# A hybrid attention and state-space layer: one Strassen group of 14 weight pairs, the second half's indexer and attention first, rotary rows gathered by head group

## The chip, the cores and the metric

The kernel runs on one core of a Trainium2 chip. The core has a matmul engine (TensorE, in the profile PE, with its weight loads as PEld), three engines for elementwise work (VectorE or DVE, ScalarE or ACT, GpSimd or POOL), a queue engine (SyncE or SP) that issues most transfers, and 16 DMA engines that carry them. The metric is the device time of one execution in microseconds; 1805.1 us is the median of three runs before the change.

## The reference

One layer over 1024 positions of width 2048. One projection `w_in` gives queries, keys, values and a gate for sparse attention, an indexer that picks 256 keys for each query, and the inputs of a Mamba-2 mixer. Both results, 1024 wide each, are concatenated and mapped by `w_out`; a residual and a layer norm end the layer.

```python
u = jnp.einsum('bsd,de->bse', h, w_in[layer])
q, k, v, z_attn, q_idx, k_idx, w_idx, z_ssd, xbc, dt_raw = _split_cols(u, IN_WIDTHS)
q, k, q_idx, k_idx = ...            # rotary on the first quarter of each head
# for each block of 128 queries:
logits = relu(einsum('bqhd,bsd->bqhs', q_idx, k_idx))      # 16 indexer heads
score = einsum('bqhs,bqh->bqs', logits, w_idx)             # masked by chunks of 64
sel = top_k(score, 256)                                    # 8 query heads, 2 key heads
o_attn = softmax_attention(q, k[sel], v[sel]) * silu(z_attn)
# the mixer: causal convolution of 4 taps, SiLU, scan in chunks, gate, RMS norm
o_ssd = _ssd_mixer(xbc, z_ssd, dt_raw, ...)
sub = jnp.einsum('bse,ed->bsd', concat(o_attn, o_ssd), w_out[layer])
h = _layer_norm(DEEPNORM_ALPHA * h + sub, ln_g[layer], ln_b[layer])
```

All is float32. The kernel reaches that precision with three matmuls in a rounded format for each product: operand = high part + low part, and high x high, high x low and low x high are summed.

## The kernel before

**Projection (T stage).** The output columns of `w_in` are cut into tiles of 128 (`ORDER`, line 53): `misc` (indexer key, weights, time steps), `qi` (indexer queries), `k`, `v`, `q`, `z`, `xbc` and `zs`. The 1024 positions are two halves `h`, the 2048 input channels two sides `u`. A *piece* is one weight tile of 128 x 1024 (one side of a column tile) times one x set of eight 128 x 512 tiles: 8 steps of 3 matmuls into a PSUM bank `pj`. A *plain* tile takes two pieces for each half, one for each side. Columns in `GROUPS` (line 56) go through Strassen's scheme in Winograd's form instead: two column tiles are one pair, and with the two halves and two sides they take 7 pieces instead of 8, at the price of sums of weights (`T3`, `T2`), of x (`M2`, `M3`, `S1`, `S4`, formed by `t_xform`, line 772, and kept in DRAM as `xf`) and of results (`t_save`, `t_u3`, `t_comb`, lines 690 to 745). `units` (line 573) lists the pieces: 13 plain tiles (`FIRST`, `PLAIN`) for half 0 and then half 1, a group of 12 pairs (k, v, q and 6 of xbc), and a group of 8 (`z`, `zs`).

**Weights.** `w_load` (line 805) brings a raw tile (512 KB) to one of five `wr` buffers. `w_split` (853) makes the high part `wh` on ScalarE and the low part `wl` on VectorE or GpSimd (`two`, 456, picks), three buffers each, or spare `s4` tiles. Where a piece needs a sum, `w_load` brings all its raw tiles and `t_wacc` (824) adds them; a sum that a later piece needs again is stored to DRAM and loaded back. `product` (656) says which: the second piece of a pair's first phase loads B12, B22 and B11 and stores T3 and T2, the next phase loads those again.

**x.** `request` and `t_xst` (751 to 770) bring and split the eight tiles of the next x set when the one before last is used up. Their raw tiles come from the `u` buffers (27 of 2 KB a partition), which everything else uses as well.

**Indexer, attention, scan.** When a column tile is done, a task takes it on: rotary by `rope_rows` (1258), on 32 rows of a tile and so once for each of 20 tiles; `t_qi` and `t_score` (1380, 1421) the indexer; `t_topk` (1442) a bitwise search for the cut, 33 counting passes on ScalarE for each block of queries; `t_kv` and `t_attn` (1613, 1649) attention in three lanes in the order of `ATT` (line 63), half 0 first; `t_ssd` and `t_gate` (1828, 1943) the scan and its norm. Each task is a generator that says at each `Need` what it waits for.

**Output (O stage).** `mixed` times `w_out`, again by Strassen: 7 products (`PRODUCTS`, line 64) of 8 pieces, 24 matmuls to a piece. Weights that are sums are added in `t_wacc` as they are loaded, T1 and T2 stored for T2 and T4. `forms` (917) loads or forms the left operands of the next product when the third of eight pieces of the current one comes. `E_ORDER` (65) puts the mixer's rows first. `t_oevac` and `ln_apply` (2034, 2125) add residuals and do the layer norm; the eight `t_fill` transfers (2120) put `ln_b` into the output beforehand, and GpSimd's accumulating transfers add to it.

**What sets the order.** The whole order is made while the kernel is built. `Flow` (342) keeps a model (`Sim`, 124) of each engine's clock and of the buffers. Matmuls are taken in the order of `units`; between them `pump` (460) issues steps of tasks whose needs the model holds for met, lower priority numbers first. Every instruction goes to its engine in that order, and each engine works through its queue strictly. All instructions are issued through one helper, so every row of the profile has line 301, and groups are told apart by tile names: `pj<-xh,wh` and the like are T pieces (x moves), `pj<-wh,xh` O pieces (weights move), `wr` raw weights, `xt` and `xf` raw x and sums of x, `t` stored sums of weights, `mx` rows of `mixed`, `s<-s,sm` softmax exponentials.

Of the kernel before, what the change touches and what calls it, by code (L numbers as in the profile page):

```python
# [29 lines left out]
NU = 27  # L30
# [3 lines left out]
XRAW = 5  # L34
# [8 lines left out]
def tile_order():  # L43
# [28 lines left out]
def tile_cols(kind, j):  # L72
    if kind == "misc":
        return [(O_KI, 64), (O_WI, 16), (O_DT, 16)]
    base = {"qi": O_QI, "k": O_K, "v": O_V, "q": O_Q, "z": O_Z}
# [48 lines left out]
class Sim:  # L124


    LAT = 70.0

    def __init__(self):
# [4 lines left out]
        self.recent = []  # L134

# [141 lines left out]
    def dma(self, eng, out, in_, kw):  # L277
        q = {"SP": "SP", "A": "AQ", "G": "G"}[eng]
        at, notes = self.deps([out], [in_], "D")
        start = max(self.clk[q], at)  # L280
        self.clk[q] = start + (1000.0 if eng == "G" else 400.0)
        sb = in_ if in_dram(out) else out
        row = max(sb.ap[-1][1] * 4, 64)
        x = max(start + (1000 if eng == "G" else 400), self.clk["D"])
        self.clk["D"] = x + max(out.size(), in_.size()) * 4 * (1 / 400 + 0.6 / row)
        cell = [self.clk["D"] + 1500.0, start]
        self.note(notes, cell, "D")
        return cell

# [52 lines left out]
class Flow:  # L342
# [6 lines left out]
    def __init__(self, nc):  # L349
# [11 lines left out]
        self.spare = 2  # L361
        self.signals = []
# [13 lines left out]
    def avail(self, tag):  # L376
        if tag == "us":
            return self.avail("u") + max(self.avail("s4") - self.spare, 0)
        if tag == "ob":
# [3 lines left out]
    def new(self, tag, shape, dtype=F):  # L383

        if tag == "us":
            tag = "u" if self.avail("u") else "s4"
        if tag == "ob":
# [27 lines left out]
    def ready(self, task):  # L415
# [10 lines left out]
        for tag, k in n.slots.items():  # L426
            if self.avail(tag) < k + (n.keep if tag == "u" else 0):
# [112 lines left out]
class Piece:  # L540


    def __init__(self, kind, h=0, t=0, u=0, **kw):
# [3 lines left out]
        self.done = self.after = None  # L547
        self.op = ALU.add
# [3 lines left out]
class Layer:  # L552
    def __init__(self, ctx, tc, a):
# [7 lines left out]
        for tag, n in (("xh", 16), ("xl", 16), ("wr", 5), ("wh", 3), ("wl", 3), ("u", NU), ("s4", N4), ("cv", 2), ("sm", 8)):  # L561
# [11 lines left out]
    def units(self):  # L573
# [3 lines left out]
        self.sets = [("x", 0, 0), ("x", 0, 1), ("x", 1, 0), ("x", 1, 1)]  # L577
# [7 lines left out]
        def plain(h, tile, u, listed=True):  # L585
            kind, j = tile
            t = ORDER.index(tile)
            p = Piece("T", h, t, u, load=(("w", t, u),), n=2 * h + u, open=u == 0, close=u == 1, key=(h, t),
# [3 lines left out]
            put(p, listed)  # L592

        for u in range(2):
            for tile in FIRST:
                plain(0, tile, u)
        for tile in PLAIN[:-3]:
            plain(0, tile, 0)
            plain(0, tile, 1)
        for u in range(2):  # L600
            for tile in PLAIN[-3:]:
                plain(0, tile, u)
        for u in range(2):
            for tile in FIRST:
                plain(1, tile, u)
        for tile in PLAIN:
            plain(1, tile, 0)
            plain(1, tile, 1)
        a11 = 2
        for gi, pairs in enumerate(GROUPS):  # L610
            base = len(self.sets)
            if gi:
                self.sets.append(("x", 1, 0))
                a11 = base
                base += 1
            self.sets += [("f", "M2"), ("f", "M3"), ("x", 0, 1), ("f", "S1"), ("f", "S4"), ("x", 1, 1)]
# [4 lines left out]
            for ph in range(3):  # L621
                for couple in couples:
                    for f in range(2):
                        for c in couple:
                            i = put(self.product(gi, c, pairs[c], ph, f, n[ph][f]))
                            if ph and not (ph == 1 and f == 1):
                                self.hooks.setdefault(max(i - 2, 0), []).append(lambda gi=gi, c=c, ph=ph, f=f: self.pre_ld(gi, c, ph, f))
# [1567 lines left out]
```

## Time and profile before

| | us |
|---|---|
| runs | 1801.65, 1805.1, 1808.22 |
| median | 1805.1 |
| the profiled execution's own time | 1807.99 |
| its span, first to last instruction | 1806.2 |
| TensorE busy in it | 1669.0 |
| mean granted TensorE clock | 0.966 of full speed |

The page gives busy time and count for each engine, the same over 40 slices of the span (45 us each), and groups of instructions, each with its total, the mean duration of one in ns, and the idle time of its engine just before it with what ended it. A matmul's own duration (about 390 ns) is longer than its distance to the next one, as they overlap; the pace has to be read from a window in which TensorE is never idle. Windows give busy time, counts, granted clock and the share of the DMA engines for stretches that the reader chooses. The chain follows the work that ended last back to the start.

### The profile page before, as it was taken

What the parts mean: (1) busy time and instruction counts of PE and PEld (TensorE: products, weight loads), DVE (VectorE), ACT (ScalarE), POOL (GpSimd) and SP (SyncE); (2) the same over time, 40 slices, a digit from 0 to 9 for tenths busy, and PEclk for the clock granted to TensorE, in tenths of its full rate; (3) what the DMA queues carried; (4) which work ended last, traced back from release to release, by engine and by line L of the source; (5) the groups of instructions that cost most, each with busy time, mean ns of one, the idle gap of its engine ahead of it and who ended that gap; (6) DMA issues with size and microseconds to landing.
All of it is one profiled execution on the core that took longest, in us unless ns stands there. A gap on an engine that the chain in (4) does not pass through costs nothing.

```text
span 1806.2 us, 24602 instructions
## 1 busy us (share of the span) xinstructions
PE 1669.0 (92%) x8044; PEld 1371.3 (76%) x8044; DVE 1337.8 (74%) x2401; ACT 1026.4 (57%) x1858; POOL 180.0 (10%) x219
## 2 busy tenths in 40 slices
PE   9997999999999989989889899999999978998895
PEld 7985877787778778768767677878888767876684
DVE  6788878887766789978876666776676467679874
ACT  5674886655557866888544654654645433531442
POOL 0000000010000000012000110002311011200224
PEclk9998999999999999999989999999999998999898
DMA  7468733876766787775678977977689896687786
GB/s 273 164 242 270 269 130 100 314 272 237 284 230 226 239 272 237 236 275 185 250 246 288 346 233 231 341 253 270 216 285 313 270 359 238 229 294 275 236 193 93
DMA packets 211648, 447.76 MB, mean 248 GB/s; under 512 B 23872, under 2 KB 63552, under 8 KB 210496
## 3 DMA queue, kind: packets, MB, share of 16 engines
q1 hardware_dynamic: 206480, 437.41, 70.6%
q0 software_dynamic: 4608, 8.39, 3.1%
q8 instruction: 63, 1.03, 0.2%
q14 instruction: 65, 0.53, 0.1%
q10 hardware_dynamic: 432, 0.39, 0.1%
HBM read 340.85 MB, written 113.64 MB: 252 GB/s over the span
## 4 chain that ended last, share of the span: by engine, by line
PE 38%; DVE 19%; DMA 17%; issue 13%; ACT 9%; SPq 2%; POOL 2%; DVEq 0%; POOLq 0%; ACTq 0%
PE pj L301 29%; DVE u L301 8%; PE a L301 7%; DMA wr<-wt 6%; ACT u L301 5%; DVE wl L301 4%; DVE wr L301 2%; ACT wh L301 2%; SPq L301 2%; DMA wr<-wo 2%; PE o L301 2%; DVE s L301 2%; DMA u<-xfM 1%; DMA u<-xn 1%; DVE xl L301 1%
## 5 line engine op out<-in xcount | busy, mean ns | idle before, releaser
L301 PE MATMUL pj<-xh,wh 128*128 128x512 f32 (+1 forms) x1512 | 598.4, 396 | 36.3 <-ACT wh L301 13.1
L301 PE MATMUL pj<-xh,wl 128*128 128x512 f32 (+1 forms) x1512 | 585.3, 387 | 2.9 <-DVE wl L301 2.9
L301 PE MATMUL pj<-xl,wh 128*128 128x512 f32 (+1 forms) x1512 | 584.5, 387 | 0.0
L301 DVE TENSOR_TENSOR wl<-wr,wh 128x1024 fp32r<-128x1024 f32 (+2 forms) x241 | 287.2, 1198 | 154.4 <-ACT wh L301 154.2
L301 PEld LDWEIGHTS pj<-xh,wh 128*128 128x128 f32 x1512 | 290.1, 192 | 93.8 <-ACT wh L301 15.9
L301 PEld LDWEIGHTS pj<-xh,wl 128*128 128x128 f32 x1512 | 289.3, 191 | 63.9 <-DVE wl L301 6.3
L301 PEld LDWEIGHTS pj<-xl,wh 128*128 128x128 f32 x1512 | 289.8, 192 | 51.0
L301 ACT ACTIVATE wh<-wr 128x1024 fp32r<-128x1024 f32 (+2 forms) x245 | 250.8, 1031 | 132.5 <-PE pj L301 81.3
L301 PE MATMUL a<-u,u 128*128 128x512 f32 (+3 forms) x680 | 164.6, 361 | 19.4 <-DVE u L301 7.4
L301 DVE TENSOR_TENSOR u<-u,u 128x512 f32<-128x512 f32 (+9 forms) x254 | 154.5, 624 | 26.7 <-DMA u<-o 7.5
L301 DVE TENSOR_TENSOR wr<-wr,wr 128x1024 f32<-128x1024 f32 x107 | 132.8, 1241 | 54.0 <-DMA wr<-wt 32.3
L301 PE MATMUL pj<-wh,xh 128*128 128x512 f32 x366 | 148.6, 406 | 17.1 <-ACT xh L301 10.3
L301 ACT ACTIVATE xh<-u 128x512 fp32r<-128x512 f32 x170 | 101.7, 624 | 100.2 <-DVE u L301 34.9
L301 PEld LDWEIGHTS a<-u,u 128*128 128x128 f32 x680 | 114.6, 195 | 55.3 <-DVE u L301 13.4
L301 PE MATMUL pj<-wl,xh 128*128 128x512 f32 x366 | 145.7, 398 | 4.8 <-DVE wl L301 4.8
L301 ACT ACTIVATE u<-s,sm 128x640 bf16<-128x640 int16 (+7 forms) x132 | 130.2, 986 | 34.2 <-DVE sm L301 31.3
L301 PE MATMUL pj<-wh,xl 128*128 128x512 f32 x366 | 145.7, 398 | 1.6 <-DVE xl L301 1.6
L301 DVE TENSOR_TENSOR xl<-u,xh 128x512 fp32r<-128x512 f32 x168 | 110.1, 694 | 31.2 <-ACT xh L301 30.9
L301 ACT ACTIVATE u<-u 128x512 f32<-128x512 f32 (+4 forms) x161 | 91.1, 577 | 58.5 <-DVE u L301 42.3
L301 ACT ACTIVATE u<-a 128x256 fp32r<-128x256 f32 (+2 forms) x145 | 49.8, 361 | 123.0 <-DVE u L301 55.6
L301 ACT ACTIVATE a<-a 128x512 f32<-128x512 f32 (+3 forms) x160 | 75.5, 502 | 42.3 <-PE a L301 40.3
L301 PEld LDWEIGHTS pj<-wh,xh 128*128 128x128 f32 x366 | 70.5, 193 | 34.3 <-ACT xh L301 11.8
(223 smaller groups left out, 2084.6 us busy)
## 6 DMA issues: line engine op xcount, KB each, us to landing
wr<-wt SPq DMA_DIRECT2D x228, 512.0 KB, 4.9
wr<-wo SPq DMA_DIRECT2D x71, 512.0 KB, 5.7
u<-xt SPq DMA_DIRECT2D x104, 256.0 KB, 5.2
u<-u SPq DMA_DIRECT2D x100, 256.0 KB, 4.5
t<-wr SPq DMA_DIRECT2D x40, 512.0 KB, 4.3
wr<-t SPq DMA_DIRECT2D x40, 512.0 KB, 4.5
u<-mx SPq DMA_DIRECT2D x39, 256.0 KB, 5.2
c<-u SPq DMA_DIRECT2D x32, 256.0 KB, 2.6
```

The costliest lines, as they stand in the source:

```text
L301: f(*args, **kw)
```

## The change

The change is large; the parts are these.

1. **Order of the T stage.** The plain part is three stages: half 0's `misc` and four `xbc` tiles; half 1's `misc`, all `qi`, all k, v, q and four `xbc`; half 0's k, v, `qi`, q. One group of 14 pairs (6 of xbc, 8 of z and zs) follows. k, v and q are now plain tiles.
2. **Attention.** `ATT` starts with half 1. The top-k of half 1 runs as two tasks of two blocks each, and attention waits for the first two masks only; masks are loaded by the lane that needs them. Attention's priorities move ahead of the scan's (2.4 to 2.6 against 3 and 4). Two key blocks are transposed and split together. `E_ORDER` is the natural order, attention rows first.
3. **Rotary.** A q tile now holds 32 rows of each of four heads, so that all rotary rows of four heads stand in one tile of 128; a k tile holds 64 rows of both heads. The rotation runs on one of four q tiles and one of two k tiles.
4. **Weights.** A group's raw tile that a later sum needs is held in its `wr` buffer after its split (`hold`, `held`); T3 = B22 - B12 is stored and T2 no longer. `wh` and `wl` have two buffers each instead of three.
5. **Early weight sums.** `t_wsum` forms T3, T1, T2 and T4 of all eight output weight tiles during the T stage and stores them; O pieces load one tile each and wait for its sum.
6. **x.** x and its sums move in pairs of tiles (`xr`, two buffers of 4 KB a partition, or `s4`), 13 sets instead of 17.
7. **Layer norm.** `t_fill` goes; `ln_b` is loaded to tiles, added in a second step on VectorE, and SP stores the output.
8. **Smaller ones.** Scratch tensors are merged, and several of their tiles move in one transfer; operands of the next product are asked for at the first piece (priority 0) and not the third; the model's DMA lands after 2500 ns instead of 1500 and has eight places in flight for each queue; `u` has 28 buffers, `sm` six.

```diff
-NU = 27
+NU = 28
-PLAIN = [("xbc", (0, 2)), ("xbc", (0, 3))] + [("qi", j) for j in range(8)]
+KVQ = [("k", 0), ("k", 1), ("v", 0), ("v", 1)] + [("q", n) for n in range(8)]
+QI = [("qi", j) for j in range(8)]
+STAGES = [
+    (0, FIRST + [("xbc", (0, 2)), ("xbc", (0, 3))], 2),
+    (1, [("misc", 0)] + QI + KVQ + [("xbc", (0, j)) for j in range(4)], 3),
+    (0, KVQ[:4] + QI + KVQ[4:], 3),
+]
 GROUPS = [
-    [(("k", 0), ("k", 1)), (("v", 0), ("v", 1))] + [(("q", n), ("q", 4 + n)) for n in range(4)]
-    + [(("xbc", (1, j)), ("xbc", (3, j))) for j in range(4)] + [(("xbc", (2, j)), ("xbc", (2, 2 + j))) for j in range(2)],
-    [(("z", n), ("zs", (n // 2, n % 2))) for n in range(8)],
+    [(("xbc", (1, j)), ("xbc", (3, j))) for j in range(4)] + [(("xbc", (2, j)), ("xbc", (2, 2 + j))) for j in range(2)]
+    + [(("z", n), ("zs", (n // 2, n % 2))) for n in range(8)],
 ]
-ATT = ((0, 0), (0, 1), (1, 0), (1, 1))
+ATT = ((1, 0), (1, 1), (0, 0), (0, 1))
-E_ORDER = list(range(8, 16)) + list(range(8))
+E_ORDER = list(range(16))
...
+    if kind == "q":
+        return [(O_Q + 128 * (j // 4 * 4 + r) + 32 * (j % 4), 32) for r in range(4)]
+    if kind == "k":
+        return [(O_K + 128 * g + 64 * j, 64) for g in range(2)]
...
-        for tag, n in (("xh", 16), ("xl", 16), ("wr", 5), ("wh", 3), ("wl", 3), ("u", NU), ("s4", N4), ("cv", 2), ("sm", 8)):
+        for tag, n in (("xh", 16), ("xl", 16), ("xr", 2), ("wr", 5), ("wh", 2), ("wl", 2), ("u", NU), ("s4", N4), ("cv", 2), ("sm", 6)):
...
+        self.hooks.setdefault(12, []).append(lambda: self.fl.add(self.t_wsum(), 6, "wsum"))
...
-                    parts = dict(T3=("B22", "B12"), T1=("B12", "B11"), T2=("B22", "T1"), T4=("T2", "B21")).get(name, (name,))
-                    keep = (("o", name, d, j),) if name in ("T1", "T2") else ()
-                    pieces.append(Piece("O", n, d, j, load=tuple(("o", x, d, j) for x in parts), keep=keep, op=ALU.subtract))
+                    pieces.append(Piece("O", n, d, j, load=(("o", name, d, j),)))
...
-        load, keep = [[((b11,), ()), ((b12, b22, b11), (t3, t2s))], [((t3,), ()), ((t2s, b21), ())],
-                      [((b11, b12), ()), ((b22,), ())], [((b21,), ())]][ph][f]
+        load, keep = [[((b11,), ()), ((b22, b12), (t3,))], [((t3,), ()), ((b11, b21), ())],
+                      [((b12, b11), ()), ((b22,), ())], [((b21,), ())]][ph][f]
+        p = Piece("T", load=load, keep=keep, n=n, open=f == 0, close=True, skip=f == 1, key=(gi, c, ph),
+                  hold=ph < 2 and f == 0, base=ph < 2 and f == 1)
...
+    def t_wsum(self):
...
+        for d in range(2):
+            for j in range(4):
+                yield Need("D", s4=4)
+                x, y, z = load("B22", d, j), load("B12", d, j), fl.new("s4", [P, 1024])
+                yield Need("V")
+                fl.two(z, x, y, ALU.subtract)
+                yield Need("")
+                fl.dma(self.tsum["T3", d, j], z)
...
-        fl.free(raw)
+        if self.late(i):
+            fl.free(raw, to="s4")
+        elif self.stream[i].hold:
+            self.held[self.stream[i].key] = raw
+            self.ev_held[self.stream[i].key].cells = [fl.cells[-1]]
+        else:
+            fl.free(raw)
...
-        if (d, j) == (0, 2) and n < 6:
+        if (d, j) == (0, 0) and n < 6:
             self.forms(n + 1)
...
     def s_q(self, h, n, x):
         fl = self.fl
-        yield from self.rope_rows(h, x)
+        if n % 4 == 0:
+            yield from self.rope_rows(h, x, "rq")
...
-        fl.stt(x, x, mv[:, 0:1], self.lnB[dc], ALU.subtract, ALU.mult)
-        yield Need("A", ev=(self.lnev[4 * h + st],))
-        fl.act(x, x, AF.Identity, scale=mv[:, 2:3])
-        yield Need("G")
+        g, b = self.lnB[dc]
+        fl.stt(x, x, mv[:, 0:1], g, ALU.subtract, ALU.mult)
+        yield Need("V", ev=(self.lnev[4 * h + st],))
+        fl.stt(x, x, mv[:, 2:3], b, ALU.mult, ALU.add)
+        yield Need()
         s0 = ROWS[h] * HALF + st * P
-        fl.nc.gpsimd.dma_start(self.a["out"][s0:s0 + P, dc * 512:(dc + 1) * 512], x, accum_op=ALU.add)
+        fl.dma(self.a["out"][s0:s0 + P, dc * 512:(dc + 1) * 512], x)
```

More of the change, by code (lines that the diff above doesn't have):

```diff
@@ L591, in plain @@
                 p.done = lambda ps: self.fl.add(getattr(self, "t_" + kind)(h, j, ps), 0, f"{kind}{j}h{h}", self.fl.t + 100)
[L592 to L609, printed above, removed]
-        for gi, pairs in enumerate(GROUPS):
[L611 to L616, printed above, removed]
+            put(p)
+        for h, tiles, end in STAGES:
+            n = len(self.sets)
+            self.sets += [("x", h, 0), ("x", h, 1)]
+            for part in [tiles[:3]] + [[t] for t in tiles[3:-end]] + [tiles[-end:]]:
+                for u in range(2):
+                    for tile in part:
+                        plain(h, tile, u, n)
+        for gi, pairs in enumerate(GROUPS):
+            a11 = len(self.sets)
+            base = a11 + 1
+            self.sets += [("x", 1, 0), ("f", "M2"), ("f", "M3"), ("x", 0, 1), ("f", "S1"), ("f", "S4"), ("x", 1, 1)]
             n = [(a11, base), (base + 1, base + 2), (base + 3, base + 4)]
@@ L766, in t_xst @@
-        fl.act(hi, raw)
-        fl.two(lo, raw, f32(hi), ALU.subtract)
-        fl.free(raw)
-        self.passing.remove(("t", n, kk))
+        k = 4 * n + kp
+        yield Need("", xs=1, ev=((self.ev_xf[kp],) if src[0] == "f" else ()))
+        raw = fl.new("xs", [P, 2, HALF])
+        fl.dma(raw, self.a["xt"][src[1], 4 * src[2] + kp] if src[0] == "x" else self.xf[src[1], kp])
+        for e in range(2):
+            yield Need("AV", ev=((self.ev_xs[k - 1],) if k > 8 else ()), xh=1, xl=1)
+            hi, lo = self.xst[n, 2 * kp + e] = fl.new("xh", [P, HALF], R), fl.new("xl", [P, HALF], R)
+            fl.act(hi, raw[:, e])
+            fl.two(lo, raw[:, e], f32(hi), ALU.subtract)
+            self.passing.remove(("t", n, 2 * kp + e))
@@ L770, in t_xst, with t_xform @@
+        fl.free(raw, to="s4" if n == len(self.sets) - 1 and kp > 1 else None)
         self.ev_xs[k].cells = [[0.0]]
-    def t_xform(self, kk):
+    def t_xform(self, kp):
         fl = self.fl
-        yield Need("", u=4, ev=(self.ev_xf[kk - 2],) if kk > 1 else ())
+        yield Need("", xr=1, s4=2, ev=(self.ev_xf[kp - 1],) if kp else ())
         x = []
-        for h, u in ((0, 0), (0, 1), (1, 0), (1, 1)):
-            x.append(fl.new("u", [P, HALF]))
-            fl.dma(x[-1], self.a["xt"][h, 8 * u + kk])
-        a, b, c, d = x
+        for tag, h, u in (("s4", 0, 0), ("s4", 0, 1), ("xr", 1, 0)):
+            x.append(fl.new(tag, [P, 2, HALF]))
+            fl.dma(x[-1], self.a["xt"][h, 4 * u + kp])
+        a, b, c = x
@@ L839, in t_wacc @@
             x = y
-        if p.keep:
+        if p.keep and len(p.keep) > 1 or p.keep and not p.base and len(parts) == 2:
             yield Need("")
@@ L1081, in start @@
                     self.emit_t(i, q)
[L1082 to L1083 removed]
+                    if q == 3:
+                        fl.free(*self.w.pop(i))
         self.nsp = nsp
@@ L1383, in t_qi @@
         s0 = 512 - n
-        yield Need("A", u=4, keep=3)
+        yield Need("A", u=4 + 2 * (("ri", h) not in self.tab), keep=3)
         cos, sin = self.table("ri", h)
@@ L1654, in load @@
             i, pr = todo.pop(0)
+            if i > 3 and i not in self.mask:
+                n = (i + 1) * P
+                m = self.mask[i] = fl.new("us", [P, 1024], BF)
+                fl.dma(m[:, 0:n], self.mask_sc[i])
+                fl.signal(self.ev_mask[i])
             rg = fl.new("us", [P, 2, P])
@@ L1900, in t_ssd @@
                     fl.signal(self.ev_h[0, g])
+            fl.free(xdd)
+            yield Need("", u=1)
+            ea = fl.new("u", [P, 2, 2, P])
+            for q in range(2):
+                for k in range(2):
+                    fl.dma(ea[64 * q:64 * q + 64, k], pairs[q, k].partition_broadcast(64))
             yield Need("A")
@@ L2087, in o_done @@
         fl = self.fl
+        if not self.ndone:
+            self.stats = fl.new("us", [P, 8, 4, 6])
         self.nc.vector.bn_stats(self.stats[:, 4 * h + st, dc], x)
```

336 lines of the change are left out of this document (191 added, 145 removed).

## The prediction

> **What bounds the kernel now.** I read the page first: busy time, slices, chain.
>
> ```profile
> PE 1669.0 (92%) x8044; PEld 1371.3 (76%) x8044; DVE 1337.8 (74%) x2401; ACT 1026.4 (57%) x1858; POOL 180.0 (10%) x219
> ...
> PE   9997999999999989989889899999999978998895
> ...
> PEclk9998999999999999999989999999999998999898
> ...
> PE 38%; DVE 19%; DMA 17%; issue 13%; ACT 9%; SPq 2%; POOL 2%; DVEq 0%; POOLq 0%; ACTq 0%
> ```
>
> TensorE is the bound: 1669.0 of 1806.2 us. It is idle for 137.2 us, and the chain shows that no single engine causes this: the steps that hold TensorE up are spread over VectorE, transfers and ScalarE. So the question is how much matmul work the change adds, and how much of the 137.2 us it returns. The windows split the span. The first answer is cut where the first output matmul starts, the second holds the stretches where the digits above dip, and one dense stretch.
>
> ```profile
> core 0: us, PE busy (x) PEld busy (x) DVE busy (x) ACT busy (x) POOL busy (x), PEclk, DMA share, GB/s
> 0.00:1338.00 1338.00, 1261.27 (x6096) 1034.92 (x6097) 1014.13 (x1833) 839.92 (x1525) 100.19 (x144) 0.97 0.72 247
> 1338.00:1806.20 468.20, 407.69 (x1950) 336.42 (x1948) 323.68 (x569) 186.51 (x333) 79.80 (x75) 0.95 0.79 250
> ```
>
> ```profile
> 100.00:160.00 60.00, 46.76 (x280) 40.24 (x279) 50.02 (x91) 32.41 (x58) 2.15 (x3) 0.89 0.79 273
> 550.00:600.00 50.00, 50.00 (x222) 41.42 (x221) 35.36 (x65) 37.74 (x62) 1.96 (x4) 1.00 0.63 211
> 881.00:1050.00 169.00, 146.21 (x716) 117.47 (x715) 119.43 (x217) 79.37 (x164) 13.64 (x17) 0.93 0.84 291
> 1430.00:1515.00 85.00, 65.75 (x280) 52.02 (x279) 57.74 (x108) 32.37 (x61) 10.22 (x10) 0.90 0.92 324
> 1600.00:1740.00 140.00, 121.39 (x515) 97.90 (x514) 121.47 (x174) 47.89 (x66) 17.74 (x19) 0.94 0.84 267
> 1786.00:1806.20 20.20, 0.75 (x4) 0.28 (x2) 4.45 (x8) 2.56 (x4) 8.09 (x9) 0.62 0.67 104
> ```
>
> At 550 to 600 us TensorE never pauses: 50.00 / 222 = 0.2252 us per matmul, the price of one below. The stretches hold the idle time in lumps: 13.2 us at 100 to 160, 22.8 at 881 to 1050, 19.3 at 1430 to 1515, 18.6 at 1600 to 1740, 19.5 after 1786. The rest, 44 us, lies thinly over 1332 us, 3.3%; I call that the usual idle share.
>
> The lumps also cost clock. Within the stretch at 1430 the matmuls behind a stall start 0.42 us apart, not 0.2252:
>
> ```profile
> 1442.90 0.63 PE L301 MATMUL pj<-wl,xh 128*128 128x512 f32 x1
> 1443.32 0.63 PE L301 MATMUL pj<-wh,xl 128*128 128x512 f32 x1
> ```
>
> The Trainium skill ("TensorE: Matmul & The Clock Gate", section "HAM oscillation — how this bites in real kernels") says that idle gaps beyond about 3.4 us put the array back to half clock; the two rows agree. By that rule a lump removed returns more than its idle time, and a lump made costs more.
>
> **The change part by part.**
>
> *Matmuls, +32.4.* A T piece is 8 k-tiles by 3 products, 24 matmuls. Before: 13 plain tiles by 2 halves by 2 sides is 52 pieces, and 20 pairs by 7 is 140: 192. After: 5, 25 and 20 plain tiles by 2 sides is 100, and 14 pairs by 7 is 98: 198. Six more by 24 by 0.2252 us is 32.4 us. All of it is on the path. Attention, indexer, scan and output products keep their matmuls.
>
> *The second group's start, -21.* At 881 us the old second group opens.
>
> ```profile
> 919.20 6.40 DMA wr<-wt
> ...
> 930.90 7.71 DMA wr<-wt
> ...
> 997.79 6.72 DMA wr<-wt
> ```
>
> These rows of the chain are weight loads that TensorE waits through: the opening pieces need one, one, three and three raw tiles out of five buffers. With one group this opening happens once, and there it is cheap (the slices from 316 us, where the first group starts, show nines). 22.8 idle less the usual 3.3% of 169 (5.6) is 17.2; the clock of 0.93 against 0.97 is 0.04 x 169 = 6.8 us, of which half speed returns half, 3.4. Together 20.6.
>
> *The first hand-over of x, -8.*
>
> ```profile
> 120.04 5.46 DMA u<-arow
> 125.52 7.48 DMA u<-xt
> ```
>
> TensorE waits behind 7.48 us for raw x, which shares the `u` buffers and the SP queue with the scan's row tables. After, x comes in pairs into its own two `xr` buffers. 13.2 less the usual 2.0 is 11.2. I take 8, as three plain stages have one hand-over more than two.
>
> *The output stage's first products, -16.* The stall at 1430 to 1515 us is, by the chain, loads of `mixed` rows and of output weights:
>
> ```profile
> 1432.82 4.80 DMA u<-mx
> 1437.70 6.97 DMA wr<-wo
> ...
> 1469.87 7.07 DMA wr<-wo
> ```
>
> They meet with attention, whose exponentials (`s<-s,sm`) run until 1586 us, 248 us into this stage:
>
> ```profile
> L301 ACT ACTIVATE s<-s,sm x64: 384/769/1163, 614.1 to 1586.1; 128x128 f32<-128x128 f32 x8, 128x256 f32<-128x256 f32 x8, 128x384 f32<-128x384 f32 x8, 128x512 f32<-128x512 f32 x8
> ```
>
> ```profile
> L301 PE MATMUL pj<-wh,xh x366: 387/389/796, 1337.9 to 1784.5; 128*128 128x512 f32 x183
> ```
>
> After, three things differ. The operand loads of the next product are asked for two pieces earlier. The T3 and T1 pieces load one finished tile each instead of two, and store nothing. And k, v, q and the second half's indexer are plain tiles of the first stages, so the large attention can start hundreds of microseconds earlier, ahead of the scan in priority, with `E_ORDER` taking attention rows first. The attention matmuls fall elsewhere at the same price. 19.3 less 2.8 is 16.5.
>
> *Weight sums and held tiles, -16 in the T stage and -9 in the O stage.*
>
> ```profile
> L301 DVE TENSOR_TENSOR wl<-wr,wh 128x1024 fp32r<-128x1024 f32 (+2 forms) x241 | 287.2, 1198 | 154.4 <-ACT wh L301 154.2
> ...
> L301 ACT ACTIVATE wh<-wr 128x1024 fp32r<-128x1024 f32 (+2 forms) x245 | 250.8, 1031 | 132.5 <-PE pj L301 81.3 <-DVE wr L301 31.8 <-issue 11.5
> ...
> L301 DVE TENSOR_TENSOR wr<-wr,wr 128x1024 f32<-128x1024 f32 x107 | 132.8, 1241 | 54.0 <-DMA wr<-wt 32.3 <-DMA wr<-wo 8.6 <-DMA wr<-ts 7.5
> ```
>
> Per pair the sums go from 4 to 5 and the 512 KB transfers from 13 to 11. Over the groups: 80 to 70 sums, 260 to 154 transfers; plain loads rise from 52 to 100. So 58 fewer, 29 MB. The x traffic falls too:
>
> ```profile
> u<-xt SPq DMA_DIRECT2D x104, 256.0 KB, 5.2
> ...
> u<-xfM SPq DMA_DIRECT2D x32, 256.0 KB, 6.4
> ```
>
> These, 32 loads of `xfS` and 32 stores are 200 issues; after, 16 first loads, 16 for four plain sets, 32 in the forming and 28 in the group make 92. Two of five raw buffers are now held until their sum, but a sum needs two new ones instead of three. The added wait is that sum's, on two landings and the held tile: behind it on VectorE stand the next splits, and TensorE waits for those. What is left of T-stage idle outside the two lumps is 76.7 - 13.2 - 22.8 = 40.7 us. Bounds: 0 and -40.7; below zero is the buffer rival. I take -16, as VectorE's idle before the sums is 54.0 us and 40 of it is transfers.
>
> The output weights' 32 sums move to `t_wsum`, lowest in priority. They and their 64 transfers lie beside T-stage matmuls, where VectorE is busy 1014.13 of 1338 us: nothing, unless the eighth set isn't ready when the O stage opens. In the O stage 16 of them belong to S2 and A22: up to 16 x 1.241 = 19.9 us out of the 121.47 of 140 at 1600 to 1740. The added bias step (below) gives part of that back. 18.6 less 4.6 is 14.0; I take 9.
>
> *Rotary, 0.* Twenty calls of a shuffle and three products become six:
>
> ```profile
> L301 DVE TENSOR_TENSOR u<-u,u 32x512 f32<-32x512 f32 x60 | 40.5, 698 | 3.9 <-DMA u<-rq 2.6
> ...
> L301 DVE STREAM_SHUFFLE u<-u 32x512 f32<-32x512 f32 x20 | 14.4, 721 | 0.0
> ```
>
> 14 x (0.721 + 3 x 0.698) = 39.4 us of VectorE goes. It lies beside matmuls, so I cost it nothing; -10 at most. The top-k in two halves repeats its small steps, likewise hidden. Splitting 13 sets of x instead of 17 is hidden too.
>
> *Layer norm and end, -8.*
>
> ```profile
> 1786.36 0.39 PE L301 MATMUL pj<-s,xl 128*128 128x512 f32 x1
> ...
> 1788.76 0.99 POOL L301 TENSOR_TENSOR mv<-mv,mhalf 128x1 f32<-128x1 f32 x1 [7.15 <-DVE mv L301]
> ...
> 1793.01 3.84 POOL L301 DMA_DIRECT2D out<-xl  x2
> ```
>
> ```profile
> L301 DVE SCALAR_TENSOR_TENSOR u<-u,mv,u 128x512 f32<-128x512 f32 x16 | 11.6, 745 | 0.0
> ```
>
> ```profile
> mx<-u SPq DMA_DIRECT2D x28, 256.0 KB, 3.5
> ```
>
> Before, ScalarE scales and POOL issues eight accumulating stores one after the other until 1796.85 us. After: the power ends at 1789.75, four bias steps of 0.745 us end at 1792.7, a store like that of `mx` lands 3.5 us later: 1796.7 instead of 1806.2, -9.5. I take -8. The eight `lnb` fills go; 32 more steps of 0.745, 23.8 us, come to VectorE.
>
> *Two split buffers instead of three, +10.* `wh` and `wl` fall from 3 to 2. A piece lasts 24 x 0.2252 = 5.4 us and its split 1.031 + 1.198 = 2.2; with two pairs the split of the next piece must fit into the piece running, with 3.2 us for whatever is queued ahead on ScalarE and VectorE; x splits and evacuations stand behind a split that waits. Bounds 0 and +73 (below). I take 10: nearly nine exposed splits at 1.1 us.
>
> **Sum.** 32.4 - 21 - 8 - 16 - 16 - 9 - 8 + 10 = -35.6: a span of 1770.6. The profiled run took 1807.99 us, 1.8 over its span; the median, 1805.1, lies 2.9 under it. 1770.6 + 1.8 - 2.9 = 1769.5; I say **1770**, 1.9% faster.
>
> **Rivals.**
>
> *The thin idle goes too: 1732.* If SP's queue is behind most of it, fewer and better spaced transfers help everywhere. For it:
>
> ```profile
> SPq L301 <- DVE u L301: 219.6, 138, 9.5
> ```
>
> Most of these are stores that sit in the queue ahead of loads. Work of 1701.4, some 20 less for a steadier clock, at 97% busy, is 1733. Against: attention and scan still interleave. The Trainium skill ("Perfetto Trace Analysis", "Identifying the Most-Contended Engine") would judge room by weight-load time: 1371.3 at the dense stretch's 41.42 of 50 is 1655, room 151 instead of 137; no term uses it.
>
> *Split buffers decide: 1833, slower.* Rows of TensorE's waits:
>
> ```profile
> PE pj L301 <- ACT wh L301: 13.1, 3, 7.0
> ...
> PE pj L301 <- DVE wl L301: 7.7, 7, 3.8
> ```
>
> A late `wl` costs 7.7 / 7 = 1.1 us. If 66 of 198 pieces are late, that is 73 us: 1770 - 10 + 73. ScalarE's 81.3 us of waiting for matmuls to free `wh` speaks for it; against it, ScalarE waited so with three pairs, and only ten splits held TensorE up. It turns the change slower from 41 late pieces on.
>
> *The output stage without filler: 1817, slower.* Between 1600 and 1740 attention is gone and a matmul takes 140 / 515 = 0.272 us. If all 1344 output matmuls run so, the stage has 62.9 us of stalls and 12 of tail, where my sum leaves 60.5 - 16 - 9 - 8 = 27.5: +47. VectorE's 87% there speaks for it; against it, the first three products have the light evacuations.
>
> *Not what it says: 1805.* Attention might still end behind the T stage, with the gains of -16 and -21 lost.
>
> **Chances.** Forecast 0.50, thin idle 0.24, split buffers 0.11, bare output stage 0.09, attention late 0.06. Range 1715 to 1832: it reaches past the fast rival by the largest unknown left there, and leaves out about half of the slowest. A measurement tells some 0.3% from no change: faster 0.73 (forecast and first rival, less 0.01 where the sum falls short), within 0.06, slower 0.21.
>
> **What would show it.** Right: no lump like 881 to 1050; softmax over before the first output matmul; fewer than ten splits awaited; the last store on SP some 10 us behind the last matmul; about 8188 matmuls. Wrong: TensorE waiting for `wh` or `wl` dozens of times; an output stage over 350 us; a drain before its first product.

## The result, and the profile after

| | before | after |
|---|---|---|
| median of four runs, us | 1806.66 | 1738.39 |
| lowest and highest, us | 1801.65, 1810.74 | 1730.81, 1741.16 |
| profiled run; its span, us | 1807.99; 1806.2 | 1736.13; 1734.3 |
| mean granted clock | 0.966 | 0.986 |

The ratio is 0.9617 [0.9575, 0.9658]: 3.8% faster, where 1.9% was forecast (1770 us). The time is inside the range and nearest to the rival "the thin idle goes too" (1732). One correction to the account of the change: in the T stage T3 is the sum B22 + B12, not a difference; only the O stage's sums subtract.

The page of the changed kernel: busy time and count of each engine, then TensorE's busy tenths and its granted clock in 40 slices (43.4 us each), then the traffic.

```profile
PE 1667.1 (96%) x8188; PEld 1380.5 (80%) x8188; DVE 1293.0 (75%) x2309; ACT 993.8 (57%) x1753; POOL 176.7 (10%) x194
...
PE   9999999999999999999999999999999979999987
...
PEclk9999999999989999999999999999999989999989
...
DMA packets 185156, 405.58 MB, mean 234 GB/s; under 512 B 19144, under 2 KB 59208, under 8 KB 185032
```

TensorE's idle time fell from 137.2 to 1734.3 - 1667.1 = 67.2 us, 70.0 less; and its busy time fell by 1.9 us although it runs 144 matmuls more, which at 0.2252 us are 32.4. So 34.3 us came back inside the busy time; most of that is clock, as worked out below. Before, ten slices had a 7 or an 8 and the last a 5; now two have a 7 or an 8, and the last a 7.

The windows of the changed kernel (columns as in the prediction: stretch, then busy us and count of PE, PEld, DVE, ACT and POOL, clock, DMA share, GB/s). The last projection matmul starts at 1368.9, the first output matmul 0.6 us later.

```profile
100.00:160.00 60.00, 57.17 (x258) 45.60 (x257) 51.84 (x89) 34.57 (x67) 0.00 (x0) 1.00 0.33 111
...
1368.90:1483.90 115.00, 102.53 (x525) 83.92 (x525) 78.17 (x130) 53.45 (x97) 4.74 (x5) 0.94 0.91 308
1483.90:1722.00 238.10, 230.01 (x1010) 189.68 (x1009) 188.80 (x269) 68.03 (x89) 23.23 (x15) 0.98 0.67 226
1722.00:1734.30 12.30, 0.40 (x2) 0.00 (x0) 8.34 (x14) 0.00 (x0) 0.98 (x1) 0.66 0.52 171
```

The whole span, cut at the last projection matmul:

```profile
0.00:1368.90 1368.90, 1334.18 (x6655) 1106.93 (x6656) 1017.70 (x1900) 872.31 (x1567) 147.78 (x173) 0.99 0.68 230
1368.90:1734.30 365.40, 332.95 (x1534) 273.60 (x1533) 275.31 (x411) 121.49 (x186) 28.95 (x21) 0.96 0.74 250
```

The T stage's idle time is 34.7 us (before: 76.7), the O stage's with its tail 32.5 (before: 60.5). Window by window the idle time reads, before and after: 13.2 and 2.8 at 100 to 160 us; 63.5 and 31.9 in the rest of the T stage; 22.4 and 12.5 in the first part of the O stage (to 1600 us before, to 1483.9 after); 18.6 and 8.1 in its later part; 19.5 and 11.9 in the tail. The gain is spread over every place where the kernel had idle time. The tail's part of it is the steadiest: from the start of the last matmul to the end, the three kernels below with the old layer norm take 19.9 to 20.4 us, the eleven with the new one 12.2 to 12.4. The O stage is 103 us shorter for a second reason: it had carried attention matmuls with it. The exponentials' row now ends ahead of the stage:

```profile
L313 ACT ACTIVATE s<-s,sm x62: 385/816/1166, 654.0 to 1279.0; 128x640 f32<-128x640 f32 x8, 128x768 f32<-128x768 f32 x8, 128x896 f32<-128x896 f32 x8, 128x1024 f32<-128x1024 f32 x8
```

TensorE's waits in the changed kernel: what was waited for, total us, times, longest.

```profile
PE a L313 <- DVE u L313: 12.6, 11, 2.5
PE pj L313 <- ACT xh L313: 10.9, 3, 7.7
PE pj L313 <- DVE xh L313: 7.2, 1, 7.2
PE pj L313 <- DVE wl L313: 5.6, 6, 1.7
...
PE pj L313 <- ACT wh L313: 2.6, 1, 2.6
```

Only seven splits are waited for, 8.2 us in all, with two buffer pairs instead of three. But spare `s4` tiles (named `s` in the profile) stand in for the third pair. The rows of the high parts that went to a spare, first before and then after:

```profile
L301 ACT ACTIVATE s<-wr 128x1024 fp32r<-128x1024 f32 x7 | 7.2, 1049 | 0.9 <-DMA wr<-wt 0.9
...
L313 ACT ACTIVATE s<-wr 128x1024 fp32r<-128x1024 f32 (+2 forms) x58 | 59.0, 1018 | 2.7 <-DMA wr<-wt 2.7
```

Seven splits took a spare before, 58 after. The longest waits left are single ones for left operands (`xh`) in the O stage.

### The profile page after: what moved, and what is told of

Same layout as the page of the kernel before. It is cut to its first block, busy times and chain, and to the rows that moved or that the text cites. A ratio compares the mean times of both kernels' runs of the same rounds, so it can differ in the third digit from the quotient of the medians.

```text
span 1734.3 us, 24108 instructions
## 1 busy us (share of the span) xinstructions
PE 1667.1 (96%) x8188; PEld 1380.5 (80%) x8188; DVE 1293.0 (75%) x2309; ACT 993.8 (57%) x1753; POOL 176.7 (10%) x194
## 5 line engine op out<-in xcount | busy, mean ns | idle before, releaser
L313 PE MATMUL pj<-xh,wh 128*128 128x512 f32 (+1 forms) x1264 | 495.9, 392 | 3.4 <-ACT u L313 3.4
L313 PE MATMUL pj<-xh,wl 128*128 128x512 f32 (+1 forms) x1264 | 486.0, 385 | 5.6 <-DVE wl L313 5.6
L313 PE MATMUL pj<-xl,wh 128*128 128x512 f32 (+1 forms) x1264 | 484.9, 384 | 0.0
L313 DVE TENSOR_TENSOR wl<-wr,wh 128x1024 fp32r<-128x1024 f32 (+1 forms) x189 | 230.5, 1220 | 179.8 <-ACT wh L313 176.7
L313 PE MATMUL pj<-xh,s 128*128 128x512 f32 (+1 forms) x640 | 204.5, 385 | 2.7 <-ACT wh L313 2.6
L313 PEld LDWEIGHTS a<-u,u 128*128 128x128 f32 x766 | 126.9, 191 | 44.8 <-DVE u L313 12.5
L313 PEld LDWEIGHTS pj<-xh,s 128*128 128x128 f32 x640 | 119.8, 191 | 25.3 <-ACT wh L313 2.8
L313 ACT ACTIVATE u<-s,sm 128x768 bf16<-128x768 int16 (+7 forms) x132 | 129.7, 983 | 15.5 <-DVE sm L313 13.5
L313 PE MATMUL pj<-xl,s 128*128 128x512 f32 (+1 forms) x320 | 121.8, 381 | 0.8 <-DVE xl L313 0.8
L313 DVE TENSOR_TENSOR u<-u,u 128x512 f32<-128x512 f32 (+7 forms) x187 | 107.6, 587 | 14.4 <-DMA u<-o 8.3
L313 DVE TENSOR_TENSOR wr<-wr,wr 128x1024 f32<-128x1024 f32 (+1 forms) x69 | 88.4, 1283 | 15.3 <-DMA wr<-wt 14.4
```

The costliest lines, as they stand in the source:

```text
L313: f(*args, **kw)
```

## The experiments

All the kernels compute the whole layer. For each, the table gives the median with its ratio to the kernel before, and from its trace: the start of the last projection matmul, where the O stage is taken to start, TensorE's idle time before and after that, and its busy time. "exp" is the start of the last softmax exponential. The kernel before ran again beside each group of these kernels, with medians from 1801.5 to 1808.65 us, so a difference of a few us between kernels is not read.

| kernel | median us | ratio, 95% | O starts | idle T | idle O | PE busy | exp |
|---|---|---|---|---|---|---|---|
| before | 1806.66 | | 1337.7 | 76.7 | 60.5 | 1669.0 | 1586.1 |
| after | 1738.39 | 0.9617 [0.9575, 0.9658] | 1368.9 | 34.7 | 32.5 | 1667.1 | 1279.0 |
| e1 slack 2500 | 1731.54 | 0.959 [0.9559, 0.9621] | 1367.7 | 37.4 | 23.0 | 1671.2 | 1324.2 |
| e9 slack 2700 | 1768.85 | 0.979 [0.9766, 0.9815] | 1377.1 | 44.0 | 40.3 | 1682.2 | 1336.0 |
| e10 margin 250 | 1735.51 | 0.9602 [0.9576, 0.9628] | 1375.0 | 37.9 | 28.6 | 1670.1 | 1285.4 |
| e8 sums at priority | 1743.24 | 0.9671 [0.9643, 0.97] | 1379.0 | 40.7 | 30.1 | 1673.3 | 1259.6 |
| e2 two groups | 1791.19 | 0.9924 [0.9895, 0.9952] | 1365.0 | 43.4 | 54.5 | 1689.2 | 1440.6 |
| e3 half 0 first | 1775.63 | 0.9838 [0.981, 0.9866] | 1311.9 | 34.6 | 50.4 | 1685.2 | 1392.2 |
| e4 no early sums | 1769.77 | 0.9804 [0.9773, 0.9835] | 1367.4 | 34.5 | 47.8 | 1680.2 | 1199.1 |
| e5 no held tiles | 1759.17 | 0.9753 [0.972, 0.9786] | 1409.4 | 56.7 | 24.0 | 1683.9 | 1266.9 |
| e6 old transfer model | 1767.58 | 0.9805 [0.9777, 0.9832] | 1401.6 | 55.0 | 28.4 | 1681.6 | 1239.5 |
| e12 earlier operands | 1729.7 | 0.957 [0.9544, 0.9596] | 1361.6 | 36.6 | 20.8 | 1665.3 | 1319.0 |
| e7 before, new model | 1792.45 | 0.9941 [0.9919, 0.9962] | 1299.0 | 61.3 | 64.6 | 1661.8 | 1556.8 |
| e11 before, early sums | 1853.55 | 1.0267 [1.0239, 1.0295] | 1322.3 | 80.6 | 103.0 | 1667.7 | 1587.6 |

**What a neutral edit does (e1, e9, e10).** The order is made by a planner from its own constants, so any edit also reshuffles it. Three kernels change only such a constant of the changed kernel.

```diff
-    SLACK = 2600.0
+    SLACK = 2500.0     # e1; 2700.0 in e9
-    MARGIN = 300.0
+    MARGIN = 250.0     # e10
```

> The changed kernel with one number of the planner moved (how far an engine may run ahead of TensorE when a task is let in, 2500 ns instead of 2600): same work, another order. Scatter theory: the order alone is worth as much as the small parts, so this moves the time by 10 us or more either way from 1738. Order theory (one group, attention out of the output stage, freed buffers): the named parts carry the gain, and this stays within 5 us of 1738, TensorE idle within 10 us of 67.

> Second control: the changed kernel with the planner's run-ahead at 2700 ns instead of 2600. Scatter theory (the undone parts cost 21 to 53 us because any disturbance of a tuned order costs that much): 1755 or more. Parts theory (they cost that because the part is missing): within 10 us of 1738, like the first control (1731.5).

> Third control: the changed kernel with the time by which the planner puts TensorE's tasks behind their operands at 250 ns instead of 300. Scatter theory: 1755 or more. Parts theory: within 10 us of 1738; a little more half clock is possible, as TensorE instructions come 50 ns nearer to their operands.

Measured against after's median: -7, +30, -3 us. e10 fits the parts theory, e1 falls between the bounds of its two theories, and e9 is beyond what its scatter theory asked for. Its span is 32.2 us longer, 24.0 of that in the O stage; its idle time is up by 9.3 us in the T stage and by 7.8 in the O stage:

```profile
0.00:1377.10 1377.10, 1333.06 (x6588) 1102.00 (x6589) 999.72 (x1877) 873.35 (x1556) 143.41 (x172) 0.99 0.66 224
1377.10:1766.50 389.40, 349.13 (x1602) 286.22 (x1600) 282.14 (x434) 129.66 (x202) 29.46 (x21) 0.94 0.75 252
```

So a difference of up to 30 us in the whole time of one undone part proves nothing by itself. What stands is the place: in all nine variants of the changed kernel that keep both held tiles and the new transfer model, idle T lies between 34.5 and 44.0 us.

**Two groups again (e2).**

```diff
-    ... for j in range(2)]
-    + [(("z", n), ("zs", (n // 2, n % 2))) for n in range(8)],
+    ... for j in range(2)],
+    [(("z", n), ("zs", (n // 2, n % 2))) for n in range(8)],
```

> The changed kernel with its 14 pairs cut into two groups, 6 of xbc and then 8 of z and zs: same matmuls, seven x sets more and a second opening. Order theory: the second opening returns as a lump of idle time of some 17 us with half clock behind it, about +21 us (1759), with a dip in the slices where the second group starts. Transfer theory (the gain is in fewer and better spaced transfers): 28 raw x transfers of 512 KB more, about +5 to +10, spread thinly. Rival: no difference, because x pairs in their own buffers arrive in time.

It costs +53 us, more than any neutral edit; 8.7 us of that is more idle time in the T stage. But not at the second opening. The windows of e2 around that (its first sums are stored from 925 us on) and behind the T stage, whose end is at 1365:

```profile
800.00:900.00 100.00, 93.91 (x447) 77.59 (x446) 82.70 (x136) 64.37 (x102) 19.30 (x26) 0.97 0.71 232
900.00:1000.00 100.00, 97.63 (x482) 80.62 (x481) 80.33 (x111) 53.23 (x85) 6.61 (x8) 1.00 0.83 283
...
1365.00:1480.00 115.00, 74.31 (x375) 57.89 (x374) 68.08 (x158) 50.81 (x127) 18.59 (x24) 0.79 0.71 238
```

The opening has 8.5 us of idle time in 200 us; the first 115 us of the O stage have 40.7, at a clock of 0.79, where after has 12.5 at 0.94. The softmax row and, from the chain of waits, what precedes the longest stall there (start, duration, what), with TensorE's row from the timeline:

```profile
L313 ACT ACTIVATE s<-s,sm x64: 385/770/1153, 654.4 to 1440.6; 128x640 f32<-128x640 f32 x8, 128x768 f32<-128x768 f32 x8, 128x896 f32<-128x896 f32 x8, 128x1024 f32<-128x1024 f32 x8
```

```profile
1449.96 1.22 PE o L313 x9
...
1452.55 6.51 DMA s<-wo
...
1459.07 5.27 DMA u<-mx
```

```profile
1466.43 0.79 PE L313 MATMUL pj<-wh,xh 128*128 128x512 f32 x1 [11.19 <-ACT xh L313]
```

Attention starts at the same time as in after (654 us) but ends 162 us later, 76 us into the O stage. Its output (`o`) must be written as rows of `mixed` and read back (`u<-mx`) before the output product that needs it; in the chain the reading stands behind a load of weights (`s<-wo`).

**Half 0's attention first (e3).** `ATT` gets its old order.

```diff
-ATT = ((1, 0), (1, 1), (0, 0), (0, 1))
+ATT = ((0, 0), (0, 1), (1, 0), (1, 1))
```

> The changed kernel with attention in the old order, half 0 first; the stages and everything else stay. Order theory: attention then starts later (half 0's indexer and queries are the last plain tiles, so about 100 us later than 646 us) and its last rows run into the output stage, which now wants attention rows first: 10 to 20 us slower, with softmax exponentials after 1369 us. Rival: attention has slack of 90 us before the output stage (its exponentials end at 1279), so nothing changes beyond scatter.

```profile
0.00:1311.90 1311.90, 1277.32 (x6175) 1055.27 (x6176) 954.13 (x1743) 817.80 (x1452) 111.66 (x153) 0.99 0.68 233
1311.90:1450.00 138.10, 105.15 (x620) 84.67 (x619) 86.45 (x208) 68.14 (x152) 21.66 (x21) 0.90 0.54 167
```

+37 us: 17.9 us more idle time, all of it in the O stage, and 18.1 us more busy time. The exponentials start at 782 us and end 80 us into the stage, and its first 138 us hold 33.0 of the 50.4 us of idle time. That looks like e2 by another cause, but it proves less. The neutral edit e9, whose last exponential starts 41 us ahead of its O stage, idles as much in the first 115 us of that stage, 25.7 us, as e3 does, 23.4:

```profile
1377.10:1492.10 115.00, 89.26 (x459) 72.10 (x458) 69.46 (x126) 50.48 (x99) 10.92 (x7) 0.85 0.87 288
```

So attention's late end is a cause in e2, by the chain and by 40.7 us; for e3 it is argued.

**No early sums (e4), sums earlier (e8), early sums on the kernel before (e11).** e4 takes `t_wsum` out and lets the O pieces add their sums as before; e8 gives `t_wsum` the priority 2.7 instead of 6; e11 adds `t_wsum` to the kernel before and lets its O pieces load finished tiles.

```diff
-        self.hooks.setdefault(12, []).append(lambda: self.fl.add(self.t_wsum(), 6, "wsum"))     # e4: out; e8: 2.7; e11: in
...
-                    pieces.append(Piece("O", n, d, j, load=(("o", name, d, j),)))                # e4: out; e11: in
...
+                    pieces.append(Piece("O", n, d, j, load=tuple(("o", x, d, j) for x in parts), keep=keep, op=ALU.subtract))   # e4: in; e11: out
...
```

> The changed kernel with the output weights' sums added as they are loaded, as before. My step: VectorE in the output stage gets 40 us back and the T1 and T2 pieces load two tiles each: +9 to +16, all of it in the output stage, which grows from 365 us. Rival: the early sums were not early (the last of the 32 is stored at 1418 us) and their traffic hurts the T stage as much as it helps: no change, or some us faster in the T stage and slower in the output stage.

> The changed kernel with the early sums ahead in priority (2.7 instead of 6), so that they can end before the output stage; in the changed kernel the last of the 32 sums is stored at 1418 us, 49 us into that stage. If the lump at 1390 to 1405 us (10 us idle, half clock behind it) comes from these late sums and their transfers: 5 to 12 us faster than 1738. Rival: their four spare tiles are then missing to attention, which ends later than 1288 us: 5 to 15 us slower.

> The kernel before with the early weight sums and nothing else of the change: the 32 sums and 64 transfers move from the output stage to the T stage. If the sums' worth (31 us when they are taken out of the changed kernel) is VectorE's load and two loads per piece in the output stage, it shows here as well: 15 us or more faster than 1803, with the output stage shorter than 468 us. If it is there only because attention no longer stands in that stage, this is within 7 us of before: attention matmuls filled the same waits.

e4's O stage, and TensorE's waits in it:

```profile
1367.40:1762.50 395.10, 347.30 (x1554) 281.25 (x1552) 311.18 (x444) 123.40 (x188) 20.31 (x18) 0.94 0.82 291
```

```profile
PE pj L313 <- DVE wl L313: 9.5, 5, 5.6
PE pj L313 <- ACT xh L313: 9.3, 2, 5.1
```

Idle O rises from 32.5 to 47.8 us with the T stage unchanged (34.5), VectorE has 35.9 us more in the stage (311.18 against 275.31), and the low parts of weights, which wait for their sum, hold TensorE up: the place is the predicted one. Between the first 115 us of the stage and the last matmul e4 idles 19.1 us, after 8.1 and the three neutral edits 2.7 to 7.0, so the place is not scatter. The +31 us is as large as e9's, so the amount is less certain.

In after itself the sums are not all early; the last is stored 49 us into the O stage:

```profile
L313 SPq DMA_DIRECT2D ts<-s x32: 319/382/922, 85.7 to 1418.0; - x32
```

I took that for the cause of the stall of 7.73 us that ends at 1404. e8 speaks against it: there the last sum is stored at 900.5 us, and the O stage still has stalls of 4.6 and 4.0 us that end at 1404 and 1411; the time is 1743.24. Its rival did not come either: attention ends earlier, not later (1259.6).

e11 was expected to gain and is 2.7% slower. One of its windows, its longest wait and the chain there:

```profile
1650.00:1760.00 110.00, 56.70 (x233) 44.37 (x232) 53.95 (x84) 30.38 (x45) 19.87 (x21) 0.73 0.64 177
```

```profile
PE o L301 <- ACT xh L301: 26.5, 1, 26.5
```

```profile
1690.24 3.21 DMA u<-xn
...
1694.26 3.12 DMA u<-xn
...
1705.15 7.89 DMA out<-xh
```

53.3 us of idle time lie in 110 us, late in the O stage. The chain there is the layer norm's: residual rows (`xn`) come one after another, then an accumulating store of 7.89 us frees the `xh` tile that the operand of the waiting matmul into `o` needs. Whether the sums delay attention or the scan by the `s4` tiles they hold was not tried; why work of theirs is still left at 1713 us stays open. What is shown: without the early sums the changed kernel idles more where the prediction put it, and with them the old kernel is slower. No neutral edit was made to the old kernel, so how much of e11's loss is its new order isn't known.

**No held tiles (e5), old transfer model (e6), new model on the kernel before (e7).** e5 loads three raw tiles for a phase's sum again and stores T2; e6 gives the planner its old transfer model, with no other change; e7 gives the new one to the kernel before.

```diff
-                ((b22, b12), (t3,))], [((t3,), ()), ((b11, b21), ())],                                       # e5
+                ((b12, b22, b11), (t3, ("s", "T2", gi, c)))], [((t3,), ()), ((("s", "T2", gi, c), b21), ())],
...
-                  hold=ph < 2 and f == 0, base=ph < 2 and f == 1)
+                  hold=False, base=False)
...
-        start = max(self.clk[q], at, lanes.pop(0))      # e6; e7 the other way
-        issue = 1000.0 if eng == "G" else 350.0
...
-        cell = [self.clk["D"] + self.LAND, start]
-        lanes.append(cell[0])
+        start = max(self.clk[q], at)
+        self.clk[q] = start + (1000.0 if eng == "G" else 400.0)
...
+        cell = [self.clk["D"] + 1500.0, start]
```

> The changed kernel without held raw tiles: a pair's second piece loads three tiles again and stores both sums, as before; 28 transfers of 512 KB more over the 14 pairs, 14 sums fewer. My step put -16 on all the traffic of the T stage together, so this part alone is about +5 to +8, in the T stage, spread thinly. Transfer theory (traffic is the main cause of the thin idle time): +20 or more. Scatter theory: within 7 us of 1738 (a moved planner number gave -7).

> The changed kernel planned with the old model of transfers (landing 1500 ns after the data, no limit of eight in flight): same work, other order. I gave this part no term. Model theory: engines and queues get instructions whose operands are not there yet, so the thin idle time returns: 20 us or more slower than 1738. Order theory: within 7 us, the scatter of a moved planner number.

> The kernel before, planned with the new model of transfers (landing 2500 ns, eight in flight) and nothing else changed. Model theory: 20 us or more faster than 1805. Order theory: within 10 us of 1805, as its lumps come from the order of the stages.

The T stage of e5:

```profile
0.00:1409.40 1409.40, 1352.71 (x6673) 1116.16 (x6674) 999.67 (x1896) 885.70 (x1592) 135.59 (x173) 0.98 0.69 237
```

and of e6:

```profile
0.00:1401.60 1401.60, 1346.58 (x6645) 1108.69 (x6646) 1016.00 (x1901) 877.67 (x1578) 146.13 (x178) 0.99 0.66 227
```

Idle T is 56.7 and 55.0 us, each some 20 above after's 34.7 and at least 11 above the highest of the nine variants. Both parts act on the T stage's idle time. Where it lies in e5 also says what the lump at the old second group was. The rows are the 100 us at the opening of the only group in after and then in e5, TensorE's largest wait in that stretch of e5, and the 100 us at the second opening in e7:

```profile
600.00:700.00 100.00, 95.67 (x462) 78.88 (x461) 81.40 (x198) 76.69 (x170) 5.67 (x6) 0.98 0.78 267
```

```profile
600.00:700.00 100.00, 85.39 (x367) 67.53 (x366) 74.39 (x183) 70.96 (x157) 11.86 (x8) 0.90 0.79 273
```

```profile
PE pj L313 <- ACT wh L313: 9.9, 3, 6.1
```

```profile
850.00:950.00 100.00, 83.97 (x386) 66.91 (x385) 77.94 (x130) 59.25 (x111) 9.91 (x13) 0.91 0.72 247
```

Without held tiles the lump is back although there is one group: 14.6 us, 12.1 of them waits for `wh` and `wl`. The ten kernels with held tiles idle 2.5 to 7.7 us from 600 to 700 us, e6 with the old model among them (5.9). The new model without held tiles (e7) leaves 16.0 us at the second opening. So in the changed kernel the held tiles make the opening cheap, not the single group and not the model. An opening without them isn't always dear: e11's second has 6.8 us.

The model alone also lowers it on the kernel before, 76.7 to 61.3 us, at a gain of 0.6% in the whole time, as idle O rises by 4.1.

**Operands asked for earlier (e12).** The two stalls that end at 1395 and 1404 us remain in after; e12 asks for the first product's operands nine pieces ahead of the stage instead of six, with e1's constant.

```diff
-    SLACK = 2600.0
+    SLACK = 2500.0
...
-        self.hooks.setdefault(self.n_t - 6, []).append(lambda: self.forms(0))
+        self.hooks.setdefault(self.n_t - 9, []).append(lambda: self.forms(0))
```

> A version meant to beat both: the changed kernel with the run-ahead of 2500 ns of the first control, and the first output product's operands asked for nine pieces before the output stage instead of six. If the lump at its opening (10 us idle and half clock in the changed kernel) is those operands' loads being asked for too late: 1722 to 1728. If they stand behind the scan's loads in SP's queue, which asking does not change, or lack free buffers: within 5 us of 1731.

e12 has to be compared with e1, which has the same constant. The first 115 us of the O stage, first in e1 and then in e12:

```profile
1367.70:1482.70 115.00, 106.88 (x550) 86.72 (x549) 77.60 (x134) 57.80 (x111) 7.20 (x5) 0.96 0.85 298
```

```profile
1361.60:1476.60 115.00, 108.35 (x569) 87.60 (x569) 79.09 (x138) 58.80 (x113) 8.61 (x6) 0.99 0.88 306
```

The idle time there is 12.5 us in after, 8.1 in e1 and 6.7 in e12, so most of the step came with the constant. By the bounds of the expectation the time, within 5 us of 1731, is the rival's: that the operands were asked for too late is not shown. 1729.7 us is the lowest median of the study, 4.3% under before, but its interval overlaps with those of after and e1, so it isn't shown to be faster than these two.

## Why the prediction was right in sign and half too small

**The clock is the mis-sized term.** The terms of idle time sum to -17.2 - 8 - 16 - 16 - 9 - 8 + 10 = -64.2, and -70.0 was measured. That they come so near is in part luck: the split term had the wrong sign, and the T stage behind the first hand-over gave -31.6 where its terms sum to -23.2. The term for the clock is 3.4 us; 34.3 came back in busy time. So some 31 of the 36 us between the predicted sum and the measured -71.9 lie there.

The trace's record of the granted clock shows most of them. In before it falls to half 19 times within the work, in after 6 times, and the time in these stretches with matmuls running went from 85.5 to 27.9 us; half of the difference, 28.8 us, is what half speed had cost. The other 5.5 us are not in that record, and where they come from stays open.

The step that failed is pricing the clock from one lump, and that one too low. A mean granted clock counts a us at half clock as half lost already, so 0.04 x 169 = 6.8 us was the loss beyond the usual share, and halving it again gave 3.4. The record has 23.9 us of half clock between 881 and 1050 (half of it is the 0.07 x 169 = 11.8 that the window shows), 19.0 of them with matmuls running: 9.5 us lost. The clocks of 0.89, 0.90 and 0.94 in the other windows had no term. One more reading was wrong: the stall ahead of the rows at 1442.90 and 1443.32 us lasted 2.89 us, so they agree with half clock, but the stall is shorter than the limit that the prediction names.

The eleven kernels with 8188 matmuls show how idle time and clock go together here. From e12 to e2, idle time goes from 57.5 to 98.0 us and busy time from 1665.3 to 1689.2: 0.59 us of busy time for each us of idle time. From before, with 32.4 us for the added matmuls (1701.4 at 137.2 us of idle), to after it is 34.3 / 70.0 = 0.49. At half a us for each, the predicted 64.2 would have given 32 us of clock and a span near 1742.

Point by point:

- *Matmuls, +32.4*: 8188, as predicted.
- *First hand-over of x, -8*: 13.2 to 2.8 us in that window, but the hand-over is no longer in it, as `xr` loads x from 35 us on. From 0 to 316 us, where both kernels have it, idle time fell from 18.9 to 5.7 us.
- *Second group's start and held tiles, -17.2 and -16, less 10 for the buffers*: the rest of the T stage gave -31.6 against -23.2. The lump is gone, and it consisted of waits for weights, as the prediction read it, but the single group did not remove it: e2 opens a second group without a lump, and e5 has one at its only opening. The held tiles did, which the prediction priced under another term; the T stage's idle time follows them and the new model (e5, e6). The transfer model had no term in my sum at all.
- *What one group is worth*: 22.0 of the 30.7 us of idle time that e2 adds lie in the O stage, into which attention was pushed, a mechanism that stood in the prediction under another term (attention out of the O stage).
- *Output stage's first products, -16*: softmax ended 90 us before the first output matmul, as predicted, but the idle time there went only from 22.4 to 12.5. What TensorE waits for there next is left operands (`xh`); why they are late stays open (e12).
- *Early sums in the O stage, -9*: 18.6 to 8.1 us; e4 shows the place.
- *End, -8*: 19.5 to 11.9 us. (In the working 1792.7 + 3.5 is 1796.2, not 1796.7.) The stores leave SP 8.5 us behind the start of the last matmul, as the timeline of after shows (start, us, engine, instruction):

```profile
1722.01 0.39 PE L313 MATMUL pj<-wr,xl 128*128 128x512 f32 x1
...
1725.22 0.98 POOL L313 TENSOR_TENSOR mv<-mv,mhalf 128x1 f32<-128x1 f32 x1 [7.45 <-DVE mv L313]
...
1730.46 0.33 SPq L313 DMA_DIRECT2D out<-xl  x1
```

- *Two split buffers, +10*: seven awaited splits, 8.2 us, where ten of 20.8 us were awaited before: a small gain, no loss. The rival "split buffers decide" fell, but its case, two pairs and nothing else, did not arise: 58 splits took a spare tile, which neither the term nor the rival had counted on.
- *Bare output stage, 1817*: it fell too. From 1483.9 to 1722 us there is no attention, and a matmul takes 238.1 / 1010 = 0.236 us, not 0.272. With VectorE at 79% of that stretch (188.80 of 238.1) the early sums and the light tail leave room.
- *The thin idle goes too, 1732*: half right. It took 20 us for the clock and 97% busy; the idle time went as in the forecast, the clock further than in the rival.

What stays open: how the 68 us divide among the parts. Undone one by one, one group, attention's order, early sums, held tiles and the model bring back 53, 37, 31, 21 and 29 us, 171 in all, more than the change gained; and a neutral constant can move the time by 30. The parts depend on each other, and the order that the planner found for after is among the better ones.

## What to carry to other kernels

Price a removed stall at its length plus what the clock loses behind it, for every stall and not just the long ones; here that was 0.4 to 0.5 us for each us of stall. Compare a combined edit with the run that shares its neutral part, as e12 with e1. When a planner writes the order, first move constants that should do nothing, and believe an undone part only where its idle time appears at a place that these do not touch. Work that others wait for must be over before the stage that reads it, and what an edit is worth in one order (the early sums) need not be what it is worth in another.

## What the runs showed of the hardware

The clock falls to half behind stalls far shorter than the lumps that the prediction counted. TensorE's rows in the timeline of before, behind a stall of 1.30 us:

```profile
1233.39 1.02 PE L301 MATMUL a<-o,u 128*128 128x1 f32 x8 [1.30 <-DVE u L301]
1234.27 0.57 PE L301 MATMUL pj<-xh,wh 128*128 128x512 f32 x1
1234.64 0.63 PE L301 MATMUL pj<-xl,wh 128*128 128x512 f32 x1
1235.07 0.63 PE L301 MATMUL pj<-xh,wl 128*128 128x512 f32 x1
```

The matmuls before the stall start 0.23 us apart, those behind it 0.43 us apart, until 1237.6, 3.4 us on. Of the 19 half-clock stretches in before, ten have no stall longer than 3.4 us in the 14 us ahead of or in them; they last 3.4 or 6.8 us, two of the others longer. The Trainium skill ("TensorE: Matmul & The Clock Gate", section "HAM oscillation — how this bites in real kernels") sets the limit at idle gaps of more than some 3.4 us; by that, these ten would not have been there. Here the measurement decides: 1.30 us with eight one-column matmuls behind it was enough. Not every short stall does it. Of the 15 stalls of 1 to 2 us in before, four were followed by half clock within 3.5 us, and of the nine of 2 to 3.4 us eight; what decides is not shown. The stretches with such short stalls alone gave back 13.2 of the 28.8 us (42.9 us of matmuls at half clock in before, 16.4 in after), those near longer stalls the rest.
